# Dropping the lock between the two block inverses, and doing both sample blocks' pooled output projection ahead of the prompt's input projection

## The chip, the core and the metric

The kernel runs on one core of a Trainium2 chip. The metric is the device time of one execution in microseconds (us); times are medians of several runs. The profiled execution is one single run, whose trace gives every instruction's start and duration.

## The reference

One encoder layer is applied to a prompt (512 tokens) and a sample (1024 tokens), with a width of 1024. Cut to what is computed:

```python
h = modulate(rmsnorm(x, n1_pre), mod[:, 0], mod[:, 1])
x = x + 0.5 * mod[:, 2] * rmsnorm(swiglu(h, f1_w1, f1_w3, f1_w2), n1_post)      # FFN 1, inner width 2816
h = modulate(rmsnorm(x, nm_pre), mod[:, 3], mod[:, 4])
z = h @ w_in                                                                     # input projection
zp = z[..., :D_POOL]
zr = token_shift(z[..., D_POOL:], shift_mu)
m = jnp.concatenate([pool_mixer(zp, pool_w, pool_scale),                         # pooled half, 512 columns
                     rwkv7_mixer(zr, w0, w2, a0, a2, g2, k_k, k_a, r_k, lnx_g, lnx_b)], axis=-1)
m = m.astype(x.dtype) @ w_out                                                    # output projection
x = x + mod[:, 5] * rmsnorm(m, nm_post)
h = modulate(rmsnorm(x, n2_pre), mod[:, 6], mod[:, 7])
x = x + 0.5 * mod[:, 8] * rmsnorm(swiglu(h, f2_w1, f2_w3, f2_w2), n2_post)       # FFN 2
```

`rwkv7_mixer` is a recurrence over time with a 64x64 state for each of 8 heads, run forward and backward (`wkv_scan`). The pooled half needs the input projection alone; the other half needs the whole recurrence.

## The kernel before

**Data and products.** Tokens go in three blocks of 512: block 0 and block 1 are the sample, block 2 is the prompt. An activation lies as 8 tiles of 128 features by 512 tokens. A product in fp32 is made of three TensorE matmuls of reduced precision: activation and weight are each split into a high and a low part, and `mm3` issues high·high, weight-high·activation-low and weight-low·activation-high into one PSUM tile. So the names are `whi`, `wlo` (weights, from the raw tile `wraw`: `whi` is a copy by ACT, `wlo` a subtraction by DVE or POOL) and `hh`, `hl` (activations). PSUM tiles are `u`, `v`, `y` (main stream), `sM` and `sb` (scan). The weight tiles come in one fixed list, `WStream`, in the order in which they are used.

**Who sets the order.** The whole program is written out at build time. Python generators issue instructions and give way between pieces; a planner (`run_until`, with the cost model `Estimate`) picks the next generator by its priority and by the time at which it takes its inputs to be ready. What results is one static list per engine. Each engine then works through its own list in order, with semaphores for the dependencies between engines, and a wait at the head of a list holds everything behind it. All instructions go through one helper (class `Queue`), so they all carry the line L161 in the profile, and are told apart by their tiles.

**Main stream.** `mainA`, `mainB`, `mainC` are one stream of dense work with the lowest claim on the engines: FFN 1 of blocks 0 and 1, the sample's input projection, and then (in `mainC`) FFN 1 of the prompt (`ffn_gen(2, 1, ..)`), the pooled output projection of block 0 (`wpool_gen([0])`), the prompt's input projection (`z_gen(0, ..)`), `wpool_gen([1])`, the other half of block 0's output projection (`wout_gen(0)`), `wpool_gen([2])`, and FFN 2 of the three blocks, into the first of which the output projections of blocks 1 and 2 are put.

- `wpool_gen([b])` takes 8 output tiles: for each, 12 matmuls from one weight tile (4 input tiles, 3 products each), a copy by ACT into a `gh` or `gl` buffer and a store by the SP queue to the scratch `wp_[b]`. Its input (`("mp", b)`, the split pooled half) is loaded by `mload_gen`.
- `wout_gen(b)` loads these stores back into `y`, adds the product of the recurrent half (`("m", b, "h")`, again by `mload_gen`), and sums squares for the norm behind it.
- `mload_gen` loads 4 tiles (`xk`, three buffers) by DMAs that the ACT queue issues, and splits each: `hh` by a copy on ACT, `hl` by a subtraction. It holds a build-time lock `norm` while it works, which `prenorm` and `post_gen` (the norms ahead of and behind each part) take as well.
- `prenorm(key, ..)` makes the split input `hh`, `hl` of the next product in two halves of 4 tiles (`h_half`): half 0 uses the buffers `hh0`, `hl0`, half 1 the buffers `hh1`, `hl1`. The pooled inputs use the same buffers: of each part given to `mload_gen` the fourth number says which half.

**Scan.** Beside the main stream, from the end of the sample's input projection on, six generators work on the recurrence. It is cut into 12 macros: macros 0 to 7 are the sample (4 pairs of heads, two halves of the tokens each), macros 8 to 11 the prompt (one per pair). Each macro has two groups, `gi` = 0 and 1. For macro `m` and group `gi`:

- `scan_prep` makes the decays, the keys and the masked product matrices (`MU`, from the PSUM tiles `sM` by a `mask` row on DVE), and sets the flag `("ba", m, gi)`. The part that overwrites the group's operands waits for the states of macro `m - 1` in that group.
- `scan_inv(sb, gi)` inverts 16 triangular blocks: two transposes in, 31 steps of a multiplication and an addition on `XN` (62 operations, for group 0 on DVE, for group 1 on POOL), transposes out, and two rounds of 16 small matmuls. Both generators take the build-time lock `inv` ahead of their first step and give it back at the end, so that in the written order one inverse ends before the next begins, whichever group it is of.
- `scan_state(sb, d)` for the directions d = 0 and 1 runs the chain of 4 chunks per group (short matmuls in `sb`, copies on ACT, the state `SBD` on DVE).
- `scan_post` norms and gates the results `yT` of a pair (rows `yT`, `pg`, `pv`) and stores them to `ms_`. After the fourth pair of a token group it sets `("m", 1)` for the sample, later `("m", 0)` for the prompt. `wout_gen` needs it.

The locks and flags exist at build time alone. On the chip remain the order of each engine's list and the semaphores that the data need.

Of the kernel before, what the change touches and what calls it, by code (L numbers as in the profile page):

```python
# [172 lines left out]
def encoder_kernel(ctx, tc, x_prompt, x_sample, c_prompt, c_sample, ada_w, ada_b, n1_pre, n1_post,  # L173
# [376 lines left out]
    def z_items(order):  # L550
        return [i for x in order if x[0] == "z" for i in cols(w_in, zcols[x[1]][2])]
# [2 lines left out]
    oA, oB = ([cols(w_out, j * P)[i] for j in range(KT)] for i in range(2))  # L554
    F1, F2 = ffn_items(f1_w1, f1_w3, f1_w2), ffn_items(f2_w1, f2_w3, f2_w2)
    at = 8 + 12 * (OUT_AT - 1)
    ws = WStream(F1 + F1 + z_items(zoS) + F1 + oA + z_items(zoP) + oA + oB + oA + F2[:at] + oB + oB + F2[at:] + F2 + F2)


    held = set()  # L560
# [6 lines left out]
    def give(k):  # L567
        held.remove(k)
# [87 lines left out]
        hh, hl = (mt([P, 4, TB], f"{t}{i}", 1, F32R, pool) for t in ("hh", "hl"))  # L656
        hbuf.setdefault(key, []).extend((hh[:, kt, :], hl[:, kt, :]) for kt in range(4))

    def prenorm(key, stat, xget, ci, g, pool=None, need=None):
        yield from take("norm")  # L660
        if xget is None:
            xget = xget_of(xs[key[1]])
        rb = bcast(stat)
        yield WAIT
        yield from take("sq")

        def scaled(kt):
            x = xget(kt)
            yield from there(x)
            t = mt([P, TB], "sq", 2)  # L670
            V.tensor_tensor(t, x, rb, ALU.mult)
            return t

        t = yield from scaled(0)
        if need:
            yield has(need)
        prev = None
        for kt in range(KT + 1):
            if kt < KT:
                if kt % 4 == 0:  # L680
                    h_half(key, kt // 4, pool)
                h = hbuf[key][kt]
                S.activation(t, t, AF.Identity, bias=coef[:, ci + 1, kt, g:g + 1], scale=coef[:, ci, kt, g:g + 1])
                S.activation(h[0], t, AF.Copy)
            if kt:
                pick().tensor_tensor(prev[1][1], prev[0], prev[1][0].bitcast(F32), ALU.subtract)
                flags.add((key, kt - 1))
            if kt < KT:
                prev = t, h
                if kt + 1 < KT:  # L690
                    t = yield from scaled(kt + 1)
            yield PIPE
        give("sq")
        give("norm")
# [589 lines left out]
    def scan_inv(sb, gi):  # L1284
# [8 lines left out]
        E = (V, G)[gi]  # L1293
        for m in range(len(macros)):
            yield has(("ba", m, gi))
            yield from take("inv")
            U = slice(gi * 16, gi * 16 + 16)
            XG = sb.MU[0:64, 2, U, 0:32]
            diag = [MA[32 * q:32 * q + 32, U, 32 * q:32 * q + 32].rearrange("p u t -> p t u") for q in range(2)]
            S.activation(XS, eye, AF.Copy)  # L1300
            for q in range(2):
                V.transpose(two(N0[32 * q:32 * q + 32]), diag[q].unsqueeze(2).to_broadcast([32, 32, 2, 16]))
            yield WAIT
            for j in range(31, 0, -1):
                lo = j // 2
                k_ = 16 - lo
                t3 = tmp[:, 0:k_ * j].rearrange("p (t s) -> p t s", s=j)
                E.tensor_tensor(t3, N0[:, j:j + 1, 0:j].to_broadcast([64, k_, j]),
                                XS[:, lo:16, j:j + 1].to_broadcast([64, k_, j]), ALU.mult)
                E.tensor_tensor(XS[:, lo:16, 0:j], XS[:, lo:16, 0:j], t3, ALU.add)  # L1310
                if j % 3 == 1:
                    yield CHAIN
            for q in range(2):
                V.transpose(diag[q].rearrange("p (t a) u -> p t a u", a=2), two(XS[32 * q:32 * q + 32]))
            V.transpose(XG[0:32], MA[0:32, U, 0:32])
            yield WAIT
            yield from banks()
            pg = pt([P, TB], "sM", 2, pool=ps)
            for u in range(16):
                mm(pg[32:64, u * 32:u * 32 + 32], MA[0:32, gi * 16 + u, 32:64], XG[0:32, u, :])  # L1320
            S.activation(XG[32:64], pg[32:64, :].rearrange("p (u i) -> p u i", i=32), AF.Copy)
            yield WAIT
            yield from banks()
            pe = pt([P, TB], "sM", 2, pool=ps)
            for u in range(16):
                mm(pe[0:32, u * 32:u * 32 + 32], XG[32:64, u, :], MA[32:64, gi * 16 + u, 32:64])
            S.activation(MA[0:32, U, 32:64], pe[0:32, :].rearrange("p (u i) -> p u i", i=32), AF.Copy)
            yield WAIT
            flags.add(("inv", m, gi))
            give("inv")  # L1330

    def scan_state(sb, d):
        AR, BKt, UV, MA, MR, SBD, PL, bank = sb.AR, sb.BKt, sb.UV, sb.MA, sb.MR, sb.SBD, sb.PL, sb.bank[d]
# [178 lines left out]
        return lambda kt: y[:, kt, :]  # L1512

    def mainC():
        yield from ffn_gen(2, 1, ("h1", 2), lambda: spawn(mload_gen([(("mp", 0), 0, 0, 0, ("z", 1))]), PRIO_NORM))
        spawn(then(has(("x2", 2), ("wp", 0)), lambda: prenorm(("hm", 2), stats[("x2", 2)], ysrc(1, 2), 3, 0)), PRIO_NORM)
        yield from wpool_gen([0])
        yield from z_gen(0, zoP, [2], [("hm", 2)], None)
        spawn(mload_gen([(("mp", 1), 1, 0, 0, ("z", 1)), (("mp", 2), 2, 0, 1, ("z", 0))]), PRIO_NORM)
        yield from wpool_gen([1])  # L1520
        spawn(mload_gen([(("m", 0, "h"), 0, 4, 0, ("m", 1))]), PRIO_NORM)
        yield from wout_gen(0)
        spawn(then(has(("x3", 0), ("wp", 2)), lambda: prenorm(("h2", 0), stats[("x3", 0)], ysrc(0, 0), 6, 1)), PRIO_NORM)
# [105 lines left out]
```

## Time and profile before

| | |
|---|---|
| median of 3 runs | 3784.26 us (3783.14 to 3785.41) |
| the profiled execution | 3780.28 us, with a span of 3778.3 us from the first instruction to the last |
| matmuls in the span | 19579 |
| mean over the span of the granted TensorE clock | 0.956 |
| instructions in the span | 53665 |

How to read the profile's rows: PE is TensorE's matmuls, PEld its weight loads, DVE is VectorE, ACT is ScalarE, POOL is GpSimd, SP is the SyncE queue, which here issues transfers only; `ACTq` is the ACT queue issuing a transfer. A row of a timeline gives start, duration, engine, line, operation, the tiles written and read, their shape, and "x" the number of like instructions in a row; in square brackets stand the idle time ahead of it and the tile that ended it. `PEclk` is the clock that TensorE was granted, as a share of full speed (in the row of 40 slices, in tenths). A table of windows gives for each stretch the busy time of each engine, the number of its instructions, the clock and what the DMA engines moved. The chain of work that ended last goes through PE nearly all the time.

By place in the program, in the trace's time: the prompt's FFN 1 runs at 1150 to 1820, block 0's pooled projection at 1820 to 1854, the prompt's input projection at 1890.6 to 2170.8, block 1's pooled projection at 2175.6 to 2230, block 0's recurrent half at 2264.7 to 2318.6, the prompt's pooled projection up to 2356.8, FFN 2 from 2406.7 to 3766.

### The profile page before, as it was taken

The numbers are of one execution on the slowest core, as the hardware profiler recorded it, in microseconds if no ns is written. First come the engines' busy times: TensorE is split into PE (matmuls) and PEld (weight loads), VectorE is DVE, ScalarE is ACT, GpSimd is POOL, SyncE is SP. The second block draws the span as 40 slices with busy tenths as digits, with TensorE's granted clock in tenths as the row PEclk, the third lists the DMA queues.
The fourth block names the chain that finished last, engine by engine and source line by source line (L and its number), as shares of the span: only waits on it lengthen the run. The fifth ranks groups of instructions, "written<-read, shape, count | busy, mean of one in ns | idle before, by whom it ended". The sixth has DMA issues, their size and how long they took to land. (4 is left out here: it accounts for less than half of the span.)

```text
span 3778.3 us, 53665 instructions
## 1 busy us (share of the span) xinstructions
PE 3593.2 (95%) x19579; PEld 2703.6 (72%) x19579; DVE 1999.0 (53%) x3801; ACT 1424.1 (38%) x2776; POOL 1410.4 (37%) x1716
## 2 busy tenths in 40 slices
PE   7999999998999999999899989799999999999998
PEld 4667878876676767666666666567787778877886
DVE  3128362237237778776777776778448622242223
ACT  3324342225335434344345433343334432234222
POOL 2333444443132222234234233432344344444444
PEclk8999999998999999999889978599999999999999
DMA  7655343334344322222324343222254333334332
GB/s 274 235 181 169 91 154 92 99 90 134 123 128 126 93 67 88 82 71 87 117 76 122 96 137 105 74 73 77 87 159 151 103 115 98 93 109 132 94 95 78
DMA packets 557980, 432.11 MB, mean 114 GB/s; under 512 B 27029, under 2 KB 511572, under 8 KB 553620
## 3 DMA queue, kind: packets, MB, share of 16 engines
q1 hardware_dynamic: 524900, 379.90, 32.8%
q10 hardware_dynamic: 32816, 48.78, 4.1%
q8 instruction: 155, 2.54, 0.3%
q14 instruction: 109, 0.89, 0.1%
HBM read 367.23 MB, written 61.34 MB: 113 GB/s over the span
## 5 line engine op out<-in xcount | busy, mean ns | idle before, releaser
L161 POOL TENSOR_TENSOR wlo<-wraw,whi 128x512 fp32r<-128x512 f32 x672 | 892.6, 1346 | 1294.2 <-ACT whi L161 866.5
L161 DVE TENSOR_TENSOR y<-y,y 128x512 f32<-128x512 f32 x480 | 327.2, 684 | 848.9 <-PE y L161 847.9
L161 ACT ACTIVATE whi<-wraw 128x512 fp32r<-128x512 f32 x938 | 559.2, 622 | 181.6 <-PE v L161 139.7
L161 PE MATMUL u<-hh,whi 128*128 128x512 f32 x1392 | 568.2, 408 | 10.2 <-ACT zraw L161 4.0
L161 PE MATMUL u<-hl,whi 128*128 128x512 f32 x1392 | 564.3, 405 | 14.1 <-POOL hl L161 7.4
L161 PE MATMUL v<-hh,whi 128*128 128x512 f32 x1392 | 562.4, 404 | 12.8 <-ACT hh L161 7.6
L161 PE MATMUL u<-hh,wlo 128*128 128x512 f32 x1392 | 567.0, 407 | 0.1
L161 PE MATMUL v<-hl,whi 128*128 128x512 f32 x1392 | 561.0, 403 | 1.0 <-DVE hl L161 1.0
L161 PE MATMUL v<-hh,wlo 128*128 128x512 f32 x1392 | 560.7, 403 | 0.0
L161 PE MATMUL y<-gh,whi 128*128 128x512 f32 x1056 | 425.6, 403 | 12.8 <-DVE y L161 10.8
L161 PE MATMUL y<-gl,whi 128*128 128x512 f32 x1056 | 422.7, 400 | 0.2 <-DVE gl L161 0.2
L161 PE MATMUL y<-gh,wlo 128*128 128x512 f32 x1056 | 422.2, 400 | 0.0
L161 POOL TENSOR_TENSOR XN<-XN 64x126 f32<-64x126 f32 (+22 forms) x744 | 322.4, 433 | 93.6 <-DVE XN L161 18.5
L161 PEld LDWEIGHTS u<-hl,whi 128*128 128x128 f32 x1392 | 266.6, 191 | 81.5 <-DVE hl L161 12.6
L161 ACT ACTIVATE gh<-s 128x512 fp32r<-128x512 f32 x132 | 83.3, 631 | 639.3 <-DVE s L161 639.3
L161 PEld LDWEIGHTS u<-hh,whi 128*128 128x128 f32 x1392 | 266.3, 191 | 80.9 <-issue 7.7
L161 PEld LDWEIGHTS v<-hh,whi 128*128 128x128 f32 x1392 | 264.2, 190 | 82.9 <-ACT hh L161 11.3
L161 PEld LDWEIGHTS u<-hh,wlo 128*128 128x128 f32 x1392 | 266.3, 191 | 68.8 <-issue 9.5
L161 PEld LDWEIGHTS v<-hl,whi 128*128 128x128 f32 x1392 | 264.4, 190 | 66.3 <-issue 4.9
L161 PEld LDWEIGHTS v<-hh,wlo 128*128 128x128 f32 x1392 | 264.8, 190 | 62.9 <-issue 5.9
L161 DVE TENSOR_TENSOR wlo<-wraw,whi 128x512 fp32r<-128x512 f32 x266 | 206.4, 781 | 150.6 <-ACT whi L161 149.8
L161 PEld LDWEIGHTS y<-gh,whi 128*128 128x128 f32 x1056 | 199.9, 189 | 67.2 <-DVE y L161 12.0
(252 smaller groups left out, 4504.6 us busy)
## 6 DMA issues: line engine op xcount, KB each, us to landing
wraw<-in_f_w_dram SPq DMA_DIRECT2D x792, 256.0 KB
ada<-in_ada_w_dram SPq DMA_DIRECT2D x32, 1024.0 KB
wraw<-in_w_in_dram SPq DMA_DIRECT2D x98, 256.0 KB
xk<-xs ACTq DMA_DIRECT2D x96, 256.0 KB
xs<-y ACTq DMA_DIRECT2D x48, 256.0 KB
wraw<-in_w_out_dram SPq DMA_DIRECT2D x48, 256.0 KB
in_k<-zk SPq DMA_DIRECT2D x48, 128.0 KB
in_kk<-zkk SPq DMA_DIRECT2D x48, 128.0 KB
```

The source lines that it names most:

```text
L161: return f(*args, **kw)
```

## The change

It does four things. The lock `inv` falls away, so that the two groups' inverses may be interleaved in the written order. `wpool_gen([1])` stands directly behind `wpool_gen([0])`, ahead of the prompt's input projection, with its weights moved to the same place in `WStream` (the sets `oA` are one and the same 8 tiles of `w_out`). To make that possible, block 1's pooled input is loaded in the same `mload_gen` as block 0's, and goes into half 1 of the `hh`, `hl` buffers in place of half 0; so the second half of the prompt's `prenorm` may be written only when `wpool_gen([1])` is done (`half2`). The `mload_gen` of block 2 keeps its place behind the input projection, where `wpool_gen([1])` no longer follows it, but block 0's `mload_gen`.

```diff
-    ws = WStream(F1 + F1 + z_items(zoS) + F1 + oA + z_items(zoP) + oA + oB + oA + F2[:at] + oB + oB + F2[at:] + F2 + F2)
+    ws = WStream(F1 + F1 + z_items(zoS) + F1 + oA + oA + z_items(zoP) + oB + oA + F2[:at] + oB + oB + F2[at:] + F2 + F2)
...
-    def prenorm(key, stat, xget, ci, g, pool=None, need=None):
+    def prenorm(key, stat, xget, ci, g, pool=None, need=None, half2=None):
...
                 if kt % 4 == 0:
+                    if kt and half2:
+                        yield has(half2)
                     h_half(key, kt // 4, pool)
...
             yield has(("ba", m, gi))
-            yield from take("inv")
             U = slice(gi * 16, gi * 16 + 16)
...
             flags.add(("inv", m, gi))
-            give("inv")
...
     def mainC():
-        yield from ffn_gen(2, 1, ("h1", 2), lambda: spawn(mload_gen([(("mp", 0), 0, 0, 0, ("z", 1))]), PRIO_NORM))
-        spawn(then(has(("x2", 2), ("wp", 0)), lambda: prenorm(("hm", 2), stats[("x2", 2)], ysrc(1, 2), 3, 0)), PRIO_NORM)
+        yield from ffn_gen(2, 1, ("h1", 2), lambda: spawn(mload_gen([(("mp", b), b, 0, b, ("z", 1)) for b in range(2)]), PRIO_NORM))
+        spawn(then(has(("x2", 2), ("wp", 0)), lambda: prenorm(("hm", 2), stats[("x2", 2)], ysrc(1, 2), 3, 0, half2=("wp", 1))), PRIO_NORM)
         yield from wpool_gen([0])
+        yield from wpool_gen([1])
         yield from z_gen(0, zoP, [2], [("hm", 2)], None)
-        spawn(mload_gen([(("mp", 1), 1, 0, 0, ("z", 1)), (("mp", 2), 2, 0, 1, ("z", 0))]), PRIO_NORM)
-        yield from wpool_gen([1])
+        spawn(mload_gen([(("mp", 2), 2, 0, 1, ("z", 0))]), PRIO_NORM)
         spawn(mload_gen([(("m", 0, "h"), 0, 4, 0, ("m", 1))]), PRIO_NORM)
         yield from wout_gen(0)
```

How the written order moves shows at two places. The first is PE ahead of the first matmul of the prompt's input projection (the last row shown). Before, 53 rows stand there behind the last of block 0's pooled projection, and all but two are the scan's (the two are the norm's sum over the squares, and its broadcast `y` from `ident` and `rstat`; a row marked x4 is four matmuls):

```order
L161 MATMUL sb_9081<-AR_9073,SBD_9077 64x64 x2
L161 MATMUL sb_9081<-MU_9075 64x64 x2
L161 MATMUL y_15927<-ident_71,rstat_15879 128x128 x4
L161 MATMUL sb_9080<-SBD_9077,AR_9073 64x128
L161 MATMUL sb_9080<-MU_9075 64x64 x2
L161 MATMUL sb_9081<-SBD_9077,AR_9073 64x128
L161 MATMUL sb_9081<-MU_9075 64x64 x2
L161 MATMUL u_15977<-hh_15936,whi_15551 128x512
```

Now, at the same place, the rows are the last of block 1's pooled projection (`u_16344`), then four rows of a state, then the input projection (`u_16468`):

```order
L161 MATMUL y_16373<-ident_71,rstat_16310 128x128 x4
L161 MATMUL sM_16380<-in_wa_16090,a2s_152 128x256
L161 MATMUL sM_16381<-in_wa_16090,a2s_152 128x256
L161 MATMUL u_16344<-hl_15351,whi_16201 128x512
L161 MATMUL sM_16395<-MU_9075 32x32 x16
L161 MATMUL u_16344<-hh_15350,wlo_16202 128x512
L161 MATMUL sb_9080<-SBD_9077,AR_9073 64x128
L161 MATMUL sb_9080<-MU_9075 64x64 x2
L161 MATMUL sb_9081<-SBD_9077,AR_9073 64x128
L161 MATMUL sb_9081<-MU_9075 64x64 x2
L161 MATMUL u_16468<-hh_16388,whi_16247 128x512
```

The norm's broadcast moved to where pooled rows still follow it, and the rows of the scan that stood alone are spread among the pooled rows. The second place is ACT where the recurrent half of block 0 is loaded for `wout_gen(0)`: `xk` from `m_177` is block 0's scratch, `m_179` the prompt's, `in_wa` and `ta` belong to `scan_prep`, `s0p` to a state. Before, block 0's load stands ahead of a state step and of `in_wa`, and the prompt's load (not shown) is long done:

```order
L161 ACTIVATE sg_19441<-sM_19444,w0h_148 128x256
L161 DMA xk_19463<-m_177 128x512
L161 DMA xk_19465<-m_177 128x512
L161 DMA xk_19467<-m_177 128x512
L161 ACTIVATE XN_9076<-sb_9080 64x128
L161 ACTIVATE s0p_19479<-SBD_9077,PL_9079 128x128
L161 ACTIVATE XN_9076<-sb_9081 64x128
L161 ACTIVATE s0p_19485<-SBD_9077,PL_9079 128x128
L161 ACTIVATE ta_19442<-sM_19487,w0h_148 128x256
```

Now the prompt's last load and its splits (`hh_19352`) stand here, and block 0's three loads behind `in_wa`:

```order
L161 ACTIVATE XN_9076<-sb_9080 64x128
L161 ACTIVATE s0p_19469<-SBD_9077,PL_9079 128x128
L161 ACTIVATE XN_9076<-sb_9081 64x128
L161 ACTIVATE s0p_19475<-SBD_9077,PL_9079 128x128
L161 ACTIVATE ta_19438<-sM_19477,w0h_148 128x256
L161 ACTIVATE ta_19438<-sM_19478,w0h_148 128x256
L161 ACTIVATE MU_9075<-sb_9080 64x128
L161 ACTIVATE hh_19352<-xk_19432 128x512
L161 ACTIVATE MU_9075<-sb_9081 64x128
L161 ACTIVATE in_wa_19273<-ta_19438,kam_150,kah_149 128x512
L161 DMA xk_19520<-m_177 128x512
L161 DMA xk_19522<-m_177 128x512
```

The prompt's load moved from under block 1's pooled projection to ahead of block 0's load, and block 0's load behind the activation `in_wa`.

## The prediction

> **What bounds the kernel now.** I read the page's first two parts, then the table of windows at the borders of stages (found by matching the program's order with the trace), then the timelines of single engines there.
>
> ```profile
> PE 3593.2 (95%) x19579; PEld 2703.6 (72%) x19579; DVE 1999.0 (53%) x3801; ACT 1424.1 (38%) x2776; POOL 1410.4 (37%) x1716
> PEclk8999999998999999999889978599999999999999
> ```
>
> PE is the bound: 95% busy. Its clock dips in slices 19 to 25 (1795 to 2455 us), so the time to win lies there. By stage:
>
> ```profile
> core 0: us, PE busy (x) PEld busy (x) DVE busy (x) ACT busy (x) POOL busy (x), PEclk, DMA share, GB/s
> 1150.00:1820.00 670.00, 643.70 (x4476) 460.52 (x4477) 493.83 (x1067) 279.85 (x614) 196.37 (x375) 0.98 0.28 84
> 1820.00:1854.00 34.00, 32.55 (x200) 23.90 (x199) 25.86 (x73) 13.65 (x33) 4.67 (x4) 1.00 0.55 170
> 1854.00:1890.60 36.60, 29.18 (x221) 21.36 (x218) 27.87 (x56) 14.56 (x34) 16.52 (x27) 0.57 0.38 116
> 1890.60:1985.00 94.40, 87.48 (x540) 59.49 (x540) 68.44 (x156) 43.45 (x96) 31.74 (x64) 0.82 0.27 77
> 1985.00:2175.60 190.60, 179.11 (x1321) 126.72 (x1319) 144.47 (x336) 87.21 (x199) 70.98 (x157) 0.96 0.37 111
> 2175.60:2230.00 54.40, 51.41 (x335) 35.49 (x336) 40.21 (x97) 22.62 (x53) 16.06 (x19) 0.84 0.40 127
> 2230.00:2264.70 34.70, 28.01 (x245) 21.45 (x245) 23.68 (x63) 12.21 (x30) 10.91 (x24) 0.67 0.45 146
> 2264.70:2356.80 92.10, 87.71 (x538) 61.23 (x536) 64.01 (x130) 35.47 (x84) 35.77 (x58) 0.85 0.33 102
> 2356.80:2406.70 49.90, 34.15 (x252) 26.40 (x251) 41.50 (x94) 15.45 (x35) 18.06 (x20) 0.58 0.31 102
> 3000.00:3377.00 377.00, 372.24 (x1620) 299.06 (x1619) 109.45 (x160) 112.80 (x199) 166.95 (x131) 1.00 0.35 103
> ```
>
> The rows are: the prompt's first FFN beside the scan; pooled projection of block 0; a gap in which the main stream has nothing (call it B); the prompt's input projection, its first 94 us and the rest; pooled projection of block 1; a second gap (D); the rest of block 0's output projection with the prompt's pooled part; a third gap; and a pure FFN stretch. B and D begin and end so:
>
> ```profile
> 1853.49 0.39 PE L161 MATMUL v<-hh,wlo 128*128 128x512 f32 x1
> ...
> 1890.57 0.79 PE L161 MATMUL u<-hh,whi 128*128 128x512 f32 x1 [0.30 <-ACT hh L161]
> ...
> 2229.59 0.40 PE L161 MATMUL u<-hh,wlo 128*128 128x512 f32 x1
> ...
> 2234.20 1.13 PE L161 MATMUL sM<-yT,center 128*128 128x256 f32 x4 [0.35 <-DVE yT L161]
> ...
> 2264.67 0.80 PE L161 MATMUL u<-hh,whi 128*128 128x512 f32 x1
> ```
>
> B ends when prenorm delivers the prompt's h, D when block 0's half of the mixer output is there: 2234.20 is the first matmul of the last scan_post of the sample group, 30.5 us ahead of wout_gen's first.
>
> Now what PE rows cost when nothing is wrong. The last window gives 377.00/1620 = 0.233 us for a 512-column matmul. The first holds 1584 of these (368.6 us) and 2892 scan rows in the other 301.4 us: 0.104 us each, usual small waits included. Against these prices:
> - B: 220 scan rows and 1 main, 23.1 us; took 36.6, so 13.5 lost.
> - First 94.4 us of the input projection: 151 main rows and 389 others, 35.2 + 40.5 = 75.7; 18.7 lost.
> - The rest to 2175.6: 329 main, 992 others, 179.8; 10.8 lost.
> - Block 1's pooled projection: 96 main, 239 others, 47.2; 7.2 lost. D: 25.5 of 34.7; 9.2 lost.
>
> B and what follows it lose 32.2 us together, at a granted clock of 0.57 and 0.82: a stretch with scan rows alone runs slow, and the slowness reaches into the stage behind.
>
> **The change part by part.**
>
> *Pooled projection of block 1 moves from behind the input projection to ahead of it.* Its 96 matmuls, 8 weight tiles (each with a split on ACT and on DVE or POOL), 8 copies and 8 stores on SP, and the load of 4 tiles on ACT are the same number; they now stand in B. That they fit there is shown by the 1820:1854 row: the same work for block 0 has PE busy 32.55 of 34.00 us with SP's stores and loads in the same pattern, so the queue past which they move (SP) delays nothing; the 8 tiles' subtractions, on POOL or DVE, move with them. I take B's and the following loss as gone: -32 us. Bounds: -32.2, and 0 if the scan, not PE, sets the pace (a rival below).
>
> *A new wait, half2.* The second half of prenorm's h may be written only after block 1's pooled projection. In the order its last matmul stands ahead of the input projection's first, so the condition holds when it is asked. Behind it on DVE and ACT stands only the rest of that prenorm. Cost 0; if a half came late, the nearest row is what the input projection waits for h already, 5.0 us:
>
> ```profile
> PE u L161 <- POOL hl L161: 5.0, 2, 3.5
> ```
>
> *The load of the prompt's pooled half (mload_gen of block 2) moves into D.* Before, it ran under block 1's pooled projection:
>
> ```profile
> 2192.17 1.29 ACTq L161 DMA_DIRECT2D xk<-m  x3
> ...
> 2221.10 0.62 ACT L161 ACTIVATE hh<-xk 128x512 fp32r<-128x512 f32 x1
> ...
> 2256.33 0.33 ACTq L161 DMA_DIRECT2D xk<-m  x1
> ...
> 2262.58 0.80 ACT L161 ACTIVATE in_wa<-ta,kam,kah 128x512 f32<-128x512 f32 x1
> 2263.29 0.62 ACT L161 ACTIVATE hh<-xk 128x512 fp32r<-128x512 f32 x1
> ```
>
> The first two rows are that load, the next one block 0's load and the last one its first tile, on which D ends. In the new order block 2's load stands first, holds "norm", and block 0's is issued only behind the `in_wa` row, which before ran at 2262.58 instead of 2256.33: 6.3 us later, plus up to four activations of 0.62 in between. I take 8 us. Also z_finish of the prompt's last pooled columns now falls among the scan_post rows on DVE; one such row group lasted 4.0 us:
>
> ```profile
> 2172.13 0.71 DVE L161 TENSOR_TENSOR gl<-gh 128x527 f32<-128x527 f32 x1 [1.46 <-ACT gh L161]
> 2172.87 2.22 DVE L161 TENSOR_TENSOR gl<-gl 128x525 f32<-128x525 f32 x3
> 2175.12 0.24 DVE L161 TENSOR_TENSOR gl<-gl,edge 128x8 f32<-128x8 f32 x2
> 2175.40 0.76 DVE L161 SCALAR_TENSOR_TENSOR gh<-gl,gh 128x512 f32<-128x512 f32 x1
> ```
>
> Together +12 us. Bounds: 0 (all under scan_post), and 29.5 + 4 = 34 (block 2's load takes as long as it did, 2192.17 to 2221.72, all of it on the path). I stay near the low end, since that scan_post's 22 us (2234.20 to 2256.33) run beside it.
>
> *No lock between the inverses.* The lock makes one inverse wait while the other works. Two places, first the first pair, then macro 8, group 0 (on DVE):
>
> ```profile
> 1241.32 1.27 DVE L161 TENSOR_TENSOR MU<-sM,mask 128x512 f32<-128x512 f32 x2
> ...
> 1250.35 1.50 DVE L161 TENSOR_TENSOR XN<-XN 64x78 f32<-64x78 f32 x6
> ...
> 1275.47 29.18 POOL L161 TENSOR_TENSOR XN<-XN 64x31 f32<-64x31 f32 x62 [9.56 <-DVE XN L161]
> ...
> 2177.36 2.49 POOL L161 TENSOR_TENSOR XN<-XN 64x45 f32<-64x45 f32 x6
> ...
> 2186.55 1.24 DVE L161 TENSOR_TENSOR MU<-sM,mask 128x512 f32<-128x512 f32 x2
> ...
> 2195.27 3.88 DVE L161 STREAM_TRANSPOSE XN<-MU 32x1024 f32<-32x1024 f32 x2
> ```
>
> The mask row ends when the input is ready. The first pair: ready at 1242.59, POOL starts at 1275.47, 33 us. Later: ready at 2187.79, DVE starts at 2195.27, 7.5 us, and POOL's loop had ended at 2179.85. So beyond the first pair the two keep out of each other's way by their own dependencies (inverse, state, next block's preparation), and the lock costs only the small end work. Until 1820 PE is full (643.70 of 670), so an earlier scan only moves main rows back: 0. But where the first pair overlaps, the loops meet in SBUF:
>
> ```profile
> L161 DVE TENSOR_TENSOR XN<-XN x744: 155/256/1376, 1217.2 to 2611.6; 64x126 f32<-64x126 f32 x18, 64x30 f32<-64x30 f32 x12, 64x56 f32<-64x56 f32 x12, 64x78 f32<-64x78 f32 x12
> L161 DVE TENSOR_TENSOR s<-s,v 128x512 f32<-128x512 f32 x132 | 89.8, 680 | 211.2 <-PE v L161 211.1
> L161 DVE TENSOR_TENSOR acc<-acc,ss 128x512 f32<-128x512 f32 x88 | 78.4, 891 | 11.8 <-ACT ss L161 9.7
> L161 POOL TENSOR_TENSOR XN<-XN 64x126 f32<-64x126 f32 (+22 forms) x744 | 322.4, 433 | 93.6 <-DVE XN L161 18.5
> ```
>
> The same 128x512 operation takes 680 ns with one input from PSUM and 891 with both from SBUF, and single XN operations reach 1376 against 256: a DVE operation then waits for one of POOL's, 0.43 us on average. Of the first DVE inverse the row at 1250.35 and one more group of six follow the point at which POOL could now start (1242.59 and its own small preparation): 12 x 0.43 = 5 us, +5 (0 to 27, all 62).
>
> The Trainium skill speaks against this part: "SBUF — State Buffer", section "Who interferes with whom", says that a VectorE instruction with two SBUF inputs and a GpSimd instruction that reads SBUF exclude each other for a whole instruction. By that rule two inverses side by side gain little; the trace agrees (891 against 680), and what it would make of the whole is the first rival.
>
> Sum: -32 + 12 + 5 = -15 us. The profiled run took 3780.28 (span 3778.3), 4 us below the median of 3784.26; the difference is applied to the median: 3769. Nothing later changes: the third gap has the same rows, and the scan's last product is ready 71 us before the sample's second output projection asks for it:
>
> ```profile
> 2711.18 1.62 POOL L161 TENSOR_TENSOR yT<-yT,pg 128x512 f32<-128x512 f32 x1
> ...
> 2784.10 0.39 PE L161 MATMUL u<-hh,whi 128*128 128x512 f32 x1
> ```
>
> **The rivals.**
>
> *The scan sets the pace, slower.* Colliding inverses keep the last state of the sample group where it was (2234) although PE could be earlier. Then the moved work fills B but D grows by as much: 0 + 12 + 5, 3801; without the first pair's 5, 3796. It decides once collisions eat the 32 us: 74 at 0.43, of the 186 operations of DVE's three inverses between 1820 and 2234. Against it: POOL's loop ended 8 us before DVE's input was ready in the rows above. For it: preparation was never far ahead.
>
> *No difference.* D's tail takes what B gives: block 2's load costs its full 29.5 + 4, so -32 + 34 + 0 to 5: 3786. For it: ACT works in order, and a tile that lands late holds the scan's copies behind it. Against it: the load starts under scan_post.
>
> *More.* The tail stays hidden (0), and the lock wait of 7.5 us on the way to macro 8 falls away: -32 - 7.5, to 3745.
>
> *The lock does nothing* is part of the forecast (its cost beyond the first pair is 0).
>
> **How the numbers follow.** Forecast (3755 to 3776): 0.42. More (below 3755): 0.17. No difference (3777 to 3791): 0.21. The scan sets the pace (above 3791): 0.20. Within 0.2% (7.6 us) is about what a measurement can't tell from no change. So faster 0.59, same 0.21, slower 0.20. The range takes in the rival on either side: 3743 to 3799; the forecast's own is 3755 to 3776.
>
> **What would show it.** Right: no gap in main rows between the pooled projections and the input projection, clock near 1 there; the last scan_post of the sample group starts some 30 us earlier than 2234; D some 45 us long, with block 2's load in it; the DVE row XN above 261 ns on average only by the first pair. Wrong: that scan_post still near 2234 (the scan's pace), or D over 60 us (the load), or PE waits on `MU` or `sM` in 1240 to 1300 well above 5 us.

## The result and the profile after

The changed kernel is slower: 3831.27 us (median of 4 runs, 3818.82 to 3836.83) against 3783.7 us of the kernel before beside it, a ratio of 1.0116 (95% interval 1.0093 to 1.0139). The forecast was 3769 us, at most 3799. The profiled execution has a span of 3835.1 us, 56.8 us more than before.

The page's first part and its row of the granted clock, after the change:

```profile
PE 3633.9 (95%) x19579; PEld 2736.6 (71%) x19579; DVE 2004.1 (52%) x3802; ACT 1428.0 (37%) x2778; POOL 1404.7 (37%) x1715
PEclk8999999998999999898979888698999999999999
```

The same number of matmuls, the same busy share of PE, 41 us more of it: PE did the same work more slowly. The clock's digits now dip already in the slices at 1534 to 1630 and 1726 to 1822 us, where before the dips began at 1795. The table of windows by stage, first of before, then of after (us, then busy time of each engine, and the granted clock as the first number behind POOL's):

```profile
1819.60:2264.70 445.10, 408.14 (x2852) 288.73 (x2850) 330.55 (x775) 194.10 (x444) 151.27 (x294) 0.86 0.37 113
2264.70:2406.70 142.00, 121.86 (x789) 87.64 (x787) 105.52 (x223) 50.92 (x119) 53.83 (x78) 0.75 0.33 102
2406.70:2998.00 591.30, 570.34 (x3316) 429.32 (x3315) 382.77 (x703) 244.18 (x490) 230.79 (x291) 0.96 0.33 102
```

```profile
1153.00:1872.00 719.00, 684.73 (x4679) 489.97 (x4680) 520.58 (x1128) 289.86 (x638) 197.74 (x374) 0.94 0.27 82
1872.20:2309.10 436.90, 399.62 (x2663) 280.94 (x2661) 315.05 (x720) 189.05 (x427) 151.48 (x301) 0.84 0.36 110
2309.10:2439.60 130.50, 113.87 (x775) 81.97 (x775) 96.87 (x216) 50.35 (x114) 41.01 (x56) 0.80 0.34 108
2439.60:3055.00 615.40, 585.62 (x3312) 443.48 (x3311) 384.16 (x706) 243.31 (x488) 236.42 (x304) 0.93 0.32 98
1966.50:2258.20 291.70, 276.60 (x1871) 192.85 (x1872) 213.71 (x504) 127.49 (x292) 85.69 (x189) 0.86 0.31 90
2258.20:2309.10 50.90, 37.45 (x268) 25.78 (x266) 37.13 (x93) 18.45 (x45) 16.56 (x31) 0.60 0.44 140
```

Stage by stage: the prompt's first FFN takes 719.0 us in place of 669.6 (1150.2 to 1819.8), +49. From there to block 0's recurrent half, with both pooled projections, the input projection and all gaps, 436.9 in place of 445.1, -8. Up to FFN 2, 130.5 in place of 142.0, -11.5. The first FFN 2, 615.4 in place of 591.3, +24. The first FFN also starts 2.7 us later; the sum, 56 us, is the span's difference but for rounding and the last stages. The last two rows are the input projection (280.2 before) and the gap D ahead of block 0's recurrent half (34.7 before).

So the large loss lies where nothing was moved by hand and where the forecast had put 0: in the FFN beside the scan's start. The time at half clock in it can be read from the clock: 2 x (1 - 0.94) x 719 = 86 us (88.7 from the events), against 2 x (1 - 0.98) x 670 = 27 us before. A half-clock stretch begins like this (PE's timeline after the change):

```profile
1554.77 0.40 PE L161 MATMUL v<-hh,wlo 128*128 128x512 f32 x1
1556.26 1.19 PE L161 MATMUL sM<-MU 32*32 32x32 f32 x32 [1.08 <-DVE MU L161]
1557.38 0.50 PE L161 MATMUL v<-hh,whi 128*128 128x512 f32 x1
1557.71 0.44 PE L161 MATMUL v<-hl,whi 128*128 128x512 f32 x1
1557.95 0.63 PE L161 MATMUL v<-hh,wlo 128*128 128x512 f32 x1
1558.38 0.63 PE L161 MATMUL v<-hh,whi 128*128 128x512 f32 x1
1558.94 1.22 PE L161 MATMUL sM<-in_wa,w2s 64*128 64x256 f32 x4
1560.09 0.79 PE L161 MATMUL v<-hl,whi 128*128 128x512 f32 x1
1560.82 1.91 PE L161 MATMUL sM<-MU 32*32 32x32 f32 x32
```

The columns are start, duration, engine, operation, tiles. An inverse's 32 small products and a wait of 1.08 us leave four 512-column matmuls in the stretch from 1554.6 to 1558.0, and from 1558 such a matmul shows 0.63 us in place of 0.40. From there PE is hardly idle; it works at half speed until 1578, 20 us in which scan rows and a few main rows alternate.

All changes of the granted clock in all traces of this case lie on one grid of 3.41 us. Sorting the stretches of that grid (1150 to 3000 us, thirteen kernels with the same work) by the number of 512-column matmuls in them gives:

| 512-column matmuls in the stretch | at full clock: stretches, of which the next is at half | at half clock: stretches, of which the next stays at half |
|---|---|---|
| 0 to 2 | 374, 187 (50%) | 656, 611 (93%) |
| 3 to 5 | 1131, 126 (11%) | 331, 241 (73%) |
| 6 or 7 | 1008, 3 (0.3%) | 99, 12 (12%) |
| 8 or more | 3366, 0 | 94, 0 |

The clock falls, but for 3 cases, behind stretches with fewer than 6 of them, and comes back as a rule behind 6 or more; at half clock no stretch held more than 8. The Trainium skill, "TensorE: Matmul & The Clock Gate", section "Part 1: The HAM clock gate (the "warmup" mystery)", has a free-running window of 3413 ns; the traces agree on the window. Its section "HAM oscillation — how this bites in real kernels" asks for no idle gaps of PE over some 3.4 us; that is not enough here, since the gap above is 1.08 us. In the prompt's first FFN, 5 of 196 stretches before and 21 of 212 after hold fewer than 3.

Few wide matmuls can mean small rows in their place, or PE standing still, and the table does not part the two. PE's busy time does. With fewer than 6 wide matmuls in it, a full-clock stretch with PE busy under 80% was followed by a fall in 273 of 372 cases, one with PE busy 95% or more in 22 of 962. In the FFN after the change the clock falls 12 times; 10 of these falls stand behind stretches in which PE was busy 21 to 74%, each with a wait of 0.9 to 3.3 us, one behind 85% and one behind a full stretch. Before, it falls 4 times, behind 37 to 71%. So it is mostly a wait of PE between small rows that goes ahead of a fall, and the small rows that then keep the clock down: of the 1180 half-clock stretches in the table, 756 have PE busy 95% or more.

### The profile page after: what moved, and what is told of

Read it like the earlier page. It is cut to its first block, busy times and chain, and to the rows that moved or that the text cites. A ratio compares the mean times of both kernels' runs of the same rounds, so it can differ in the third digit from the quotient of the medians.

```text
span 3835.1 us, 53671 instructions
## 1 busy us (share of the span) xinstructions
PE 3633.9 (95%) x19579; PEld 2736.6 (71%) x19579; DVE 2004.1 (52%) x3802; ACT 1428.0 (37%) x2778; POOL 1404.7 (37%) x1715
```

## The experiments

Each ratio is against the kernel before run beside it on the same chip (its median there 3784 to 3790 us). The FFN and its time at half clock are those of the one profiled execution of each. "Rows" are the scan's PE rows written ahead of that FFN's last, "grouped" those in groups of 16 or more with no main row between.

| kernel | ratio (95% interval) | FFN us | at half clock us | rows | grouped |
|---|---|---|---|---|---|
| before | | 669.6 | 27.3 | 1497 | 430 |
| after | 1.0116 (1.0093 to 1.0139) | 719.0 | 88.7 | 1602 | 556 |
| e1: move alone, lock kept | 1.0014 (1.0001 to 1.0026) | 671.2 | 27.3 | 1500 | 430 |
| e2: no lock alone | 1.0109 (1.0087 to 1.0130) | 717.2 | 88.7 | 1604 | 556 |
| e3: a planner constant | 1.0037 (1.0023 to 1.0051) | 674.9 | 34.1 | 1504 | 402 |
| e4: lock for the loop alone | 1.0068 (1.0042 to 1.0093) | 705.2 | 78.5 | 1594 | 586 |
| f1: after, main first below 6 | 1.0097 (1.0069 to 1.0125) | 689.2 | 54.3 | 1494 | 385 |
| f2: before, main first below 4 | 1.0074 (1.0047 to 1.0102) | 657.7 | 13.7 | 1472 | 396 |
| f3: lock for macro 0 alone | 1.0049 (1.0033 to 1.0065) | 685.1 | 30.7 | 1602 | 448 |
| f4: e1, prompt's load late | 1.0030 (1.0013 to 1.0047) | 679.2 | 51.2 | 1500 | 430 |
| g1: no lock for macro 0 alone | 1.0076 (1.0059 to 1.0092) | 710.7 | 73.7 | 1578 | 511 |
| g2: after, lock for macro 0 | 1.0076 (1.0049 to 1.0102) | 694.2 | 53.9 | 1608 | 448 |
| g3: after, lock for macros 0 to 3 | 1.0063 (1.0044 to 1.0082) | 658.0 | 20.5 | 1450 | 408 |
| h1: after, 350 unread matmuls in the FFN | 1.0167 (1.0152 to 1.0182) | 736.1 | 10.2 | 1602 | 556 |
| h2: before, 183 in the gaps | 1.0005 (0.9990 to 1.0020) | 669.1 | 30.7 | 1497 | 430 |
| h3: after, 129 in the gaps | 1.0125 (1.0108 to 1.0143) | 710.9 | 68.3 | 1602 | 556 |
| h4: e1, 177 in the gaps | 1.0023 (1.0007 to 1.0039) | 672.3 | 27.3 | 1500 | 430 |

How far one profile can be trusted: e1 and f4 have the same written order in that FFN, and differ by 8 us and by 24 us at half clock; f3 and g2 by 9 and 23. After, e2 and h3, also alike there, lie at 719, 717 and 711.

### Which half of the change costs

e1 puts the lock back into the changed kernel; e2 takes it out of the kernel before:

```diff
             yield has(("ba", m, gi))
+            yield from take("inv")      # e1, in the changed kernel; e2 takes this line out of the kernel before
...
             flags.add(("inv", m, gi))
+            give("inv")                 # likewise
```

> The changed kernel with the lock put back: only the pooled projection of block 1 is moved. Theory L (the lock's absence carries the loss, by a written order in which the prompt's first FFN runs more often at the half clock): near the kernel before, 3770 to 3790 us, and the first FFN of the prompt lasts 665 to 675 us as before, against 719 in the changed kernel. Theory M (the move carries it, the half-clock time of the closed gap turns up in the input projection): 3815 to 3840 us. Theory O (the order of before is a lucky one, and every new order costs): 3810 to 3830 us, with the loss in the first FFN too.

> The kernel before with only the lock taken out: the pooled projection of block 1 stays where it was. Theory L: 3820 to 3840 us, the prompt's first FFN about 719 us as in the changed kernel (its written order there is the same), time at the half clock in it some 89 us against 27. Theory M: 3780 to 3795 us. Theory O: 3810 to 3830 us.

e1 came to 1.0014, e2 to 1.0109. The loss is the missing lock's, theory L; the move alone gains nothing (by its interval it costs 0.01 to 0.26%). Their first FFNs in the table of windows:

```profile
1150.70:1821.70 671.00, 643.28 (x4481) 460.60 (x4482) 500.07 (x1073) 282.75 (x620) 198.38 (x376) 0.98 0.29 86
```

```profile
1150.80:1868.00 717.20, 684.58 (x4681) 491.53 (x4681) 518.75 (x1127) 288.54 (x635) 199.42 (x375) 0.94 0.27 81
```

### Is it the lock, the loops, or any other order

e3 changes `AFTER_STATE = 200` to 150 in the kernel before, e4 gives the lock back ahead of the end of an inverse:

```diff
                 if j % 3 == 1:
                     yield CHAIN
+            give("inv")
             for q in range(2):
                 V.transpose(diag[q].rearrange("p (t a) u -> p t a u", a=2), two(XS[32 * q:32 * q + 32]))
...
             flags.add(("inv", m, gi))
-            give("inv")
```

> The kernel before, lock and place kept, with one planner constant changed (AFTER_STATE 150 in place of 200), so that the written order of the scan differs in many places by a little: a control for the luck of an order. Theory L: within 10 us of the kernel before, 3774 to 3794 us. Theory O: 3805 to 3830 us, with half-clock time in the first FFN of 60 us or more.

> The kernel before with the lock given back ahead of the end of an inverse: the 31 steps on DVE and on POOL still keep apart, only the transposes and the small products at the end may meet the next inverse. Its written order has in the prompt's first FFN as many scan rows in groups of 16 or more as the changed kernel (586 against 556, 430 before). Theory L in the form that the groups of scan rows on PE bring the clock down: 3815 to 3840 us. Theory L in the form that the two loops meet (SBUF, DVE's list): 3778 to 3792 us. Theory O: 3810 to 3830 us.

e3 lost 0.37%, more than L allowed and less than O: a part of any new order's loss is just that before's order is a good one. All twelve other written orders tried here (h1 to h4 aside) came out slower, by 0.14 to 1.2%. e4 lost 0.68%, with 705 us and 78 us at half clock in the FFN, though its loops on DVE and POOL keep apart in the written order. So the loss doesn't need the loops to meet; the kernel's 3813 us lies in theory O's range, and 2 us below that of the groups. The loops' own times say the same. The first fence is DVE's group over the whole run after the change, the second POOL's row on its page, the third and fourth the first DVE loop alone, before and after:

```profile
L161 DVE TENSOR_TENSOR XN<-XN x744: 153/256/1358, 1219.9 to 2650.8; 64x126 f32<-64x126 f32 x18, 64x30 f32<-64x30 f32 x12, 64x56 f32<-64x56 f32 x12, 64x78 f32<-64x78 f32 x12
```

```profile
L161 POOL TENSOR_TENSOR XN<-XN 64x126 f32<-64x126 f32 (+22 forms) x744 | 318.5, 428 | 212.6 <-DVE XN L161 155.2
```

```profile
L161 DVE TENSOR_TENSOR XN<-XN x62: 155/260/1215, 1217.2 to 1257.3; 64x126 f32<-64x126 f32 x6, 64x30 f32<-64x30 f32 x4, 64x56 f32<-64x56 f32 x4, 64x78 f32<-64x78 f32 x4
```

```profile
L161 DVE TENSOR_TENSOR XN<-XN x62: 156/272/477, 1219.9 to 1268.3; 64x126 f32<-64x126 f32 x6, 64x30 f32<-64x30 f32 x4, 64x56 f32<-64x56 f32 x4, 64x78 f32<-64x78 f32 x4
```

The three numbers behind the count are the shortest, median and longest duration in ns. DVE's median is 256 ns as before, POOL's mean 428 against 433. In the first pair, now side by side, DVE's median is 272 and its longest 477 (260 and 1215 before), while the loop takes 48 us in place of 40. Its own operations sum to 17.2 us in place of 16.3, and what DVE does between them to 32.2 in place of 24.6 (44 operations in place of 39): most of the difference lies between them, in DVE's list. The whole-instruction exclusion that the prediction took from the Trainium skill ("SBUF — State Buffer", section "Who interferes with whom") as a rival's ground shows a small price at most in these loops: 0.9 us for DVE's first and 2.3 us for POOL's (26.7 in place of 24.4), both likewise in e2 and absent in e1.

### The first pair or the later ones

f3 keeps the lock for macro 0 alone, g1 for all others; g2 and g3 put it back into the changed kernel for macro 0 and for macros 0 to 3:

```diff
-            yield from take("inv")
+            if m == 0:                  # f3, g2; g1: if m; g3: if m < 4
+                yield from take("inv")
...
-            give("inv")
+            if m == 0:                  # likewise
+                give("inv")
```

> The kernel before with the lock kept for the first macro alone. Its written order has in the prompt's first FFN as many scan rows as without the lock (1601 against 1604; 1497 before), but fewer in groups of 16 or more (448 against 556; 430 before). Theory density (more scan rows per main matmul bring the clock down): the FFN lasts 710 us or more, with 80 us or more at the half clock. Theory groups (it is their bunching): 685 to 700 us, under 55 us at the half clock. Theory first pair (the two first inverses side by side make the loss): 680 to 690 us, and the kernel at 3785 to 3800 us.

> The kernel before with the lock taken out for the first macro alone and kept for the other eleven: the reverse of the run that kept it for the first macro alone. Theory first pair (the loss in the prompt's first FFN comes from the two first inverses side by side, which shift the scan's start and everything written behind it): that FFN lasts 700 us or more, with over 60 us at the half clock, and the kernel 3810 us or more. Theory later pairs (it comes from the lock's absence at the other macros): 670 to 690 us, and the kernel under 3800 us.

> The changed kernel with the lock put back for the first macro alone: scan rows as far ahead at the end of the prompt's first FFN as in the changed kernel (3191 rows up to there against 3186, 3081 before), without that FFN's loss. Theory first pair and pace (the moved projection can only gain where the scan is ahead): the FFN about 685 us, the gap ahead of block 0's recurrent half about 40 us (106 scan rows) in place of 84 with the lock, the kernel at 3765 to 3785 us, below both. Rival, order (each new order loses half-clock time somewhere, here in the input projection): the FFN 685 us, but the input projection 285 us or more, and the kernel at 3795 to 3815 us.

> The changed kernel with the lock put back for macros 0 to 3. Its written order has in the prompt's first FFN fewer scan rows in groups of 16 or more (408 against 556 in the changed kernel and 430 before), but 242 scan rows stand alone ahead of block 0's recurrent half, as with the full lock (245). Theory groups and pace: the FFN at 655 to 670 us, the gap at 75 to 90 us, the kernel at 3775 to 3795 us. Rival, order: 3800 to 3820 us, with the FFN over 680 us.

```profile
1152.30:1837.40 685.10, 660.59 (x4677) 474.14 (x4678) 528.39 (x1128) 288.00 (x637) 198.83 (x378) 0.98 0.28 84
```

```profile
1151.20:1861.80 710.60, 675.95 (x4629) 483.62 (x4629) 524.57 (x1127) 287.60 (x630) 197.49 (x376) 0.95 0.27 81
```

The first row is f3, the second g1. f3 has the scan as far ahead as the kernel without the lock (1602 rows) and yet the clock of before: density falls. Theory first pair holds for the FFN; theory groups fits it as well, and f3 does not part the two. g1 is its mirror: the lock missing at the first macro alone brings 74 us at half clock. So one pair written side by side at the start shifts everything behind it into another order, here one with more grouped scan rows. For the kernel as a whole first pair did not hold: f3 came to 3805 us, since what it saved in the FFN it lost in the next stages (its gap B lasts 49.5 us). g2, the combination that should have beaten both kernels, failed in the same way, as the rival "order" said: the input projection took 309.5 us at a clock of 0.83. g3 had the shorter FFN that was expected, but an input projection of 286 us, and came to 3809 us in place of 3775 to 3795.

### Is the half clock the cause

f1 and f2 add a rule to the planner: while the scan runs, main is taken first when fewer than 6 (f1, changed kernel) or 4 (f2, kernel before) of its matmuls were written in the last 3.41 us of planned time.

```diff
                 p_ = min(now, key=lambda q: q.prio)
+                main = [q for q in now if q.prio == 3]
+                if scanning and main and sum(t > clock - 3413.0 for t in est.wide) < KEEP:
+                    p_ = main[0]
...
```

(`est.wide` is the list of the planned times of the 512-column matmuls; the lines that keep it are left out.)

> The changed kernel (no lock, both pooled projections ahead) with one rule more in the planner: while the scan runs, the main stream is taken first whenever fewer than 6 of its 512-column matmuls were written into the last 3.41 us of the planner's clock. The work is the same. Theory L, clock (without the lock the scan's short matmuls fill whole stretches of 3.41 us, and the clock halves): the time at the half clock in the prompt's first FFN falls from 89 to under 45 us, the FFN from 719 to 670 to 685 us, and the kernel to 3780 to 3805 us. Rival, loops (the inverses of the two groups hinder each other on DVE and POOL): both loops stay as free to meet as they were, the FFN stays at 705 us or more and the kernel above 3815 us.

> The kernel before (lock and place kept) with the same rule at 4 matmuls in place of 6: does holding the clock gain by itself. Theory L, clock: the half-clock time in the prompt's FFN, in the input projection and in the first FFN 2 falls below the 27, 49 and 46 us of before, but the scan runs later, and the gaps behind the input projection take some of it back: 3765 to 3790 us. If no more than luck of the order is at work: 3790 to 3810 us, as with the planner's other constant.

Both FFNs got shorter, 719 to 689 and 669.6 to 657.7, with less time at half clock (f1's still above the 685 and 45 us that theory clock allowed), and both kernels missed their totals: f1 spent 338.5 us in the input projection, f2 71 in block 0's recurrent half. The rule holds the scan back, and the scan comes due later. But these were new orders again. Nor is grouping the whole of it: f1 has the fewest grouped rows of all and 54.3 us at half clock. Over the thirteen orders, 85 of the 88 falls in this FFN stand behind stretches with PE busy less than 95%. h1 keeps the changed kernel's order row by row and adds matmuls that nothing reads, into a tile that the scan's own products then overwrite:

```diff
+        if tag == "sM" and scanning and ("x2", 2) not in flags:
+            for _ in range(2):
+                T.eng.matmul(o.rearrange("p (a f) -> p a f", f=P), wz, wz.unsqueeze(1).to_broadcast([P, 4, P]), ..)
...
```

(`wz` is a copy of the identity in one tile.)

> The changed kernel, with the order of all its rows kept, and 350 matmuls of 512 columns more that nothing reads: two ahead of each of the scan's `sM` tiles in the prompt's first FFN. At 0.22 us each they are 76 us of TensorE time at full clock. Theory clock (too few 512-column matmuls in a stretch of 3.41 us bring the clock down, and that is the loss): the time at the half clock in that FFN falls from 89 us to under 30, and the FFN grows by 30 to 50 us in place of 76 (749 to 769 us). Rival (the half clock goes with the order for another reason, or costs nothing by itself): the half-clock time stays above 60 us, or the FFN grows by 75 us or more (794 us and up).

```profile
1153.00:1889.00 736.00, 720.24 (x4993) 526.15 (x4994) 521.30 (x1128) 290.03 (x638) 197.26 (x374) 0.99 0.27 80
```

Of the 350 added matmuls 316 run in this FFN in the profile, 74 us at the prediction's 0.233. They made it 17 us longer (736 against 719), less than the 30 to 50 us that theory clock had expected, and the clock rose from 0.94 to 0.99; 10 us are left at half clock, and 4 of 216 stretches hold fewer than 3 wide matmuls. The kernel came to 3850 us, 19 above the changed one. So 57 us were paid back: 78 us less at half clock are worth half, 39 us, and PE stands idle for 15.8 us in place of 34.3, which is another 18 us. With the order held, work that raises the clock is mostly paid back: the half clock is the larger part of the FFN's loss. The added rows fill PE's waits at the same time, so h1 does not show what either would do alone.

### Does the clock set the gaps too

The forecast took B's and D's losses as the clock's. h2, h3 and h4 fill time in the gaps that the planner holds for idle with the same kind of matmul:

```diff
                 p_ = min(live, key=lambda q: q.ready)
-                est.free["T"] = p_.ready
+                if scanning and gap:
+                    warm(p_.ready - clock)      # one matmul for each 235 ns of 0.9 of the idle time
+                est.free["T"] = max(p_.ready, est.free["T"])
...
```

> The kernel before, with 183 matmuls of 512 columns that nothing reads put in the gaps where the main stream waits (ahead of the prompt's input projection, of block 0's recurrent half, of FFN 2), in time that the planner takes for idle. Theory clock: the time at the half clock in and right behind these gaps (31, 23 and 43 us in the gaps, 49, 25 and 46 in the stages behind) falls by more than half, the gaps shorten by 5 to 15 us each, and the kernel comes to 3735 to 3770 us. Rival pace (the gaps last as long as the scan's chain through DVE, ACT and POOL takes, whatever the clock): the gaps stay within 4 us, only the stages behind gain a little, 3770 to 3785 us. If the added rows hold up the scan's: 3790 us or more.

> The changed kernel with 129 such matmuls in its gaps (ahead of block 0's recurrent half and of FFN 2). Theory clock: 10 to 30 us below the changed kernel, 3800 to 3820 us; the prompt's first FFN stays at about 719 us. Rival pace: 3820 to 3835 us.

> The kernel with the lock and only the pooled projection moved, with 177 such matmuls in its gaps, most of them in the one ahead of block 0's recurrent half (84 us, 38 of them lost to half-clock rows). Theory clock: that gap falls to 55 to 70 us and the kernel to 3745 to 3775 us, below the kernel before. Rival pace: the gap stays at 78 us or more, 3780 to 3795 us.

> The kernel with the lock and only the pooled projection moved, with the prompt's pooled load (mload_gen of block 2) put behind block 0's. Theory pace (after the move the main stream waits 84 us for the scan's states and scan_post, ahead of block 0's recurrent half): that gap stays at 75 to 90 us, the kernel within 10 us of 3790. Theory load (block 2's load ahead of block 0's holds the gap open): the gap falls to 50 to 65 us, the kernel by 15 to 30 us.

f4 puts the prompt's load behind block 0's: `spawn(then(has((("m", 0, "h"), 3)), lambda: mload_gen([(("mp", 2), ..)])))`. The gaps in the table of windows: h2's B and D, then D of e1, of h4, and of f4:

```profile
1856.10:1892.20 36.10, 35.26 (x281) 24.62 (x280) 28.72 (x56) 16.09 (x40) 18.25 (x30) 0.95 0.40 119
2227.50:2264.80 37.30, 34.45 (x303) 24.73 (x302) 26.59 (x74) 11.84 (x30) 9.54 (x21) 1.00 0.40 123
```

```profile
2172.20:2256.20 84.00, 59.28 (x468) 43.15 (x467) 62.69 (x165) 24.23 (x59) 21.75 (x30) 0.61 0.29 88
```

```profile
2176.30:2260.40 84.10, 77.05 (x585) 54.41 (x585) 62.58 (x165) 24.41 (x59) 19.43 (x27) 0.92 0.28 85
```

```profile
2196.00:2284.10 88.10, 70.99 (x546) 51.59 (x546) 67.12 (x170) 27.32 (x69) 24.07 (x46) 0.60 0.27 86
```

B at a clock of 0.95 in place of 0.57 lasts 36.1 us in place of 36.6; D at 1.00 in place of 0.67, 37.3 in place of 34.7; e1's D at 0.92 in place of 0.61, 84.1 in place of 84.0. The shorter gaps that theory clock forecast did not come, and rival pace's did: by it, the gaps last as long as the scan's chain through DVE, ACT and POOL. Of the totals h3's (3831) lies in pace's range, h2's (3786.7) and h4's (3799.1) lie 2 and 4 us above it. Theory load fails too (88 us with the load out of the way).

How far this shows the chain is another question, for the added matmuls take PE's time themselves. In h2's B they are 60, 14 us at 0.233, as much as the 28 us less at half clock are worth, and PE is busy for 35.3 of 36.1 us. So filling these gaps did not shorten them; how long B would be at full clock without the added rows was not shown. For D it speaks for the chain that in h4 the groups of added rows, with the waits behind them, take 43 us, and in an estimate only some 12 of these passed with the next scan row's operands already there (counted from the last instruction on another engine that wrote one of its tiles, by name). In h2's B it was 10 of 19 us.

## Why the prediction was wrong, step by step

- **"Until 1820 PE is full, so an earlier scan only moves main rows back: 0."** This step failed, and holds nearly all of the loss, 49 us. 105 more scan rows stand in the FFN, which are 203 more matmuls in the trace (4679 against 4476). Neither their number nor the prediction's price of 0.104 each (21 us) gives the 49: PE is idle for 34.3 us in place of 26.3, which is 8; 61 us more at half clock are worth half, 31; and 10 are left for the added matmuls. That a full PE could be full at half speed, and that waits of 1 to 3 us could bring this on, was not in the working, though the prediction's table shows the FFN's clock (0.98) and B's (0.57) two rows apart.
- **"So the lock costs only the small end work."** On the chip, right: in both kernels the loops of the two groups alternate, and after the change only those of the first pair overlap, by 16 us. But the lock also shapes the written order, and that was where it mattered; f3 and g1 put most of the FFN's part on macro 0 alone.
- **First pair, +5 by collisions in SBUF.** The term was too large, and not the one that mattered: the first loop's operations sum to 0.9 us more, and DVE's 744 operations to 195.1 us against 194.4. The first state starts at 1285.0 in place of 1270.6, 14 us later (2.7 of them since the FFN starts later), since the first loop is spread out on DVE (rows above).
- **B and what follows, -32.** Half of the mechanism held: B is gone (3.4 us), its clock no longer matters. The gain failed, since the scan sets the pace. In e1, where the lock doesn't blur it, D grew from 34.7 to 84.0 and the whole stretch gained 10.6 us (434.5 against 445.1), which the first FFN 2 then lost again (606.3 against 591.3, with 3381 matmul records against 3316). The forecast named this rival, but let it hang on collisions; none was needed. The last scan_post of the sample starts at 2234.20 before. In e1 block 1's pooled projection was done ahead, and the input projection ended at 2172.2 (2170.8 before), so that PE was free for the scan 58 us sooner (2230.0 before), yet

```profile
L161 PE MATMUL sM<-yT,center x4: 521/634/634, 2229.5 to 2230.8; 128*128 128x256 f32 x4
```

  it starts at 2229.5, only 5 us earlier.
- **D's tail, +12.** About right for the changed kernel: from the last scan_post (2266.2) to block 0's recurrent half (2309.1) 43 us, against 30.5 before.
- **"Nothing later changes."** Failed: the first FFN 2 is 24 us longer, at a clock of 0.93 in place of 0.96, with the scan's last state at 2745.5 in place of 2697.8. By the clock that is 86 us at half clock in place of 47 (2 x 0.07 x 615 and 2 x 0.04 x 591), so some 20 of the 24 us. In e2 that stage takes 599 us, so the missing lock alone explains 8 of it; why the two changes together cost the rest is not settled.
- **The rival that ended slower** had the right side, 3801 us, by the wrong mechanism, and lacked the FFN; that it ended on the slower side is luck. Its 3801 also lay outside the stated range, which ends at 3799, though the text says that the range takes in the rival on either side.

Open: why one pair at the start leaves an order with more grouped rows and more waits for hundreds of us (it was shown, not explained), how long the gaps would be at full clock without added rows, and how much of the 1.2% any other order would have cost: e1 and e3, which leave that FFN's order nearly as it was, give 0.1 to 0.5%.

## What to carry to other kernels

Where small matmuls share PE with wide ones, "PE is 95% busy" is no bound: read the granted clock of the stage, look for PE's waits of a microsecond or more among small rows, and ask how many wide matmuls each few microseconds hold in the written order. A gap at a low clock is not yet a gap because of the clock: if the chain that ends it runs through other engines, moving work into it can move the gap to the next place where the main stream catches up with that chain, as from B to D in e1. And a planner's lock or constant is to be judged by the order that it writes; a change without it needs a control with another order, since a well-chosen one is itself worth some tenths of a per cent.

## What the runs showed of the hardware that was not expected

The clock fell behind waits of PE much shorter than the 3.41 us of a stretch, 0.9 to 3.3 us in this FFN, where small rows stood around them. Half of the full-clock stretches with fewer than 3 wide matmuls were followed by a fall, none of 3366 with 8 or more; behind stretches with PE busy 95% or more it fell in only 22 of the 316 cases. It came back as a rule behind 6 or more wide matmuls, so that small rows kept it down with PE busy. The columns that all matmuls of a stretch stream, wide and small, sort the falls more sharply than the wide ones alone: below 2500 columns 218 of 229 full-clock stretches were followed by a fall, from 3600 on 3 of 5130. And 316 matmuls of no use, 74 us of work, made the FFN only 17 us longer, since they held the clock up and filled waits. In the gaps of the kernel before such matmuls cost nothing (1.0005, 0.9990 to 1.0020), and gained nothing.
